# First attention: projections on 512 columns, queries and keys of two heads side by side

## The chip, the cores and the metric

The kernel runs on one core of a Trainium2 chip. The metric is the device time of one execution in microseconds (us). The inputs are in HBM at the start, and the result is in HBM at the end.

## What is computed

Two transformer blocks on 512 tokens of width 1024 in float32. The first block has a differential attention, a SwiGLU, a gated convolution and a second SwiGLU; the second block has windowed attention, an mLSTM and a mixture of experts. The change touches only the first block's attention:

```python
def diff_attention(x, w_qkv, w_o, ...):              # 512 x 1024, H = 8 heads, Dh = 64
    qkv = einsum('bsd,de->bse', x, w_qkv)            # 1024 x 3072: q, k, v
    q, k = partial_rotary(q) * Dh ** -0.5, partial_rotary(k)
    for each block of 128 queries:
        s = einsum('bqhcd,bkhcd->bhcqk', q, k)       # two score maps per head (c = 0, 1)
        p = softmax(where(mask, s, -1e30))           # causal by chunks of 64 keys
        o = einsum('bhqk,bkhe->bqhe', p[c=0] - lam * p[c=1], v)
    o = rms_norm(o, g_sub) * (1 - lam_init)
    return einsum('bse,ed->bsd', o, w_o)
```

## The kernel before

Tokens lie in NT = 4 tiles of P = 128, the width in KD = 8 tiles of 128 (k-tiles). A float32 product is made of three matmuls on rounded parts: `mm3` (lines 129 to 131) multiplies low by high, high by low and high by high. `split` (lines 64 and 65) makes the parts: ScalarE (ACT) writes the high part, VectorE (DVE) the low part.

Weights come through the class `Weights`. A plan lists pieces of 1 MB (a few are smaller) in the order of their use. `load` issues the DMA of a piece on SyncE's queue (SP; line 86), the first piece in two halves of four k-tiles; `prepare` splits it in two halves; `get` hands out a piece and starts what comes next: the following piece is loaded and split, the one after that loaded. Each of `raw`, `whi` and `wlo` has two buffers.

In the projections the tokens are the stationary operand of the matmul and the weights the moving one. `proj_tm` takes a piece of eight k-tiles and 256 columns, and for each token tile runs 8 x 3 matmuls of 256 columns into one PSUM tile `pq`, which ACT then copies out. One token tile of one piece is a *part*, one yield of the generator. `proj_v(c)` projects the values of heads 2c and 2c + 1 (line 383 copies them out), `proj_qk(pair)` first the queries and then the keys of two heads (line 390), each followed by `rotary` on DVE (lines 378 to 380). The tile of the queries has two buffers, that of the keys one.

The attention is a generator, `attend`. A unit is one head and one token tile of queries; there are 32. `head_start(h)` transposes the keys and queries of a head on TensorE (PE; line 397, `ptk` and `ptq`) and splits them; `head_scores` makes both score maps (line 426), their maxima and exponents; `head_turn` transposes the weights (line 449); `head_values` multiplies by the values (line 457); `head_norm` and `head_out` finish a head. Each yield is a *step*; there are 97. After the first two units there are three steps to a unit: the scores of unit i, the values of unit i - 2, the turn of unit i - 1. Counted from unit 0, unit i is thus scored in step 3i - 2 (i of 2 or more), and the scores of a head's third unit also start the next head. Heads 2 and 4 begin with steps 22 and 46 (units 8 and 16), and step 64 is the third unit of head 5 (unit 22). A head has four units, with 128, 256, 384 and 512 keys.

`weave` mixes two generators in given shares. `ATT_WEAVE` has pairs (parts, steps): so many parts of the chain `fill` (the remaining projections, then the first half of the output projection `wo`) are spread among so many steps of `attend`. The framework's scheduler keeps this order as a priority: an instruction that it holds to be ready goes ahead of an earlier one that is not. Inside `manual_schedule` PE keeps the program's order. PSUM has eight banks: four with the tag `g` for projections, four with the tag `m` for the attention. The scratch of `rotary`, the tile `vraw` of `load_vectors` (transposed at line 200 into `vps`) and the tiles of `make_bias` (line 219, `bps`) share the two buffers of the tag `pr1`.

The order before is: v(0), q(0), k(0); the constants (`vps`, `bps`); then attention, woven with q(1), k(1), v(1), q(2), k(2), v(2), q(3), k(3), v(3) and `wo`; then the second half of the output projection and all that follows.

Of the kernel before, what the change touches and what calls it, by code (L numbers as in the profile page):

```python
# [9 lines left out]
F32 = mybir.dt.float32  # L10
# [4 lines left out]
AF = mybir.ActivationFunctionType  # L15
# [6 lines left out]
P = 128  # L22
T = 512
NT = T // P
D = 1024
KD = D // P
# [9 lines left out]
def bcast_rows(ap_1d, n, rows=P):  # L36

    return bass.AP(tensor=ap_1d.tensor, offset=ap_1d.offset, ap=[[0, rows], [1, n]])
# [3 lines left out]
def blocks_kernel(ctx: ExitStack, tc: tile.TileContext, a, out):  # L42
    nc = tc.nc
    dve = nc.vector
    act = nc.scalar
# [12 lines left out]
    def pbank(tag, name="pb"):  # L58
        return psum.tile([P, T], F32, tag=tag, name=name)


    def split(hi, lo, src):

        act.activation(hi, src, AF.Copy)  # L64
        dve.tensor_tensor(out=lo, in0=src, in1=hi.bitcast(F32), op=ALU.subtract)  # L65

    class Weights:
# [9 lines left out]
        def load(self, i):  # L77
            if i < len(self.plan) and i not in self.raw:
                src, kt, cols, gain = self.plan[i]
                raw = ring.tile([P, kt, cols], F32, tag="raw", name="raw")  # L80
                if callable(src):
                    src(raw)
                else:

                    for k0, k1 in ((0, kt // 2), (kt // 2, kt)) if i == 0 else ((0, kt),):
                        nc.sync.dma_start(raw[:, k0:k1], src[k0 * P:k1 * P].rearrange("(k p) c -> p k c", p=P))
                if gain is not None:
                    nc.gpsimd.tensor_tensor(out=raw, in0=raw, in1=gain().unsqueeze(2).to_broadcast([P, kt, cols]),
                                            op=ALU.mult)
                self.raw[i] = raw  # L90
# [21 lines left out]
    W = Weights()  # L112
# [10 lines left out]
    def run(gen):  # L123
        for _ in gen:
            pass

    def mm3(ps, ah, al, bh, bl, start, stop):

        pe.matmul(ps, al, bh, start=start, stop=False)  # L129
        pe.matmul(ps, ah, bl, start=False, stop=False)  # L130
        pe.matmul(ps, ah, bh, start=False, stop=stop)  # L131
# [28 lines left out]
    def load_xt(t):  # L160

        nc.sync.dma_start(X[:, t, :], a["c_xt"][t])
# [4 lines left out]
    def new_xt():  # L167
        return (keep.tile([P, KD, T], F32R, tag="xh", name="xh"),
                keep.tile([P, KD, T], F32R, tag="xl", name="xl"))
# [105 lines left out]
    def plan_out(w, nk, first=None):  # L275
        for half, pp in enumerate(out_parts(nk)):
            for k0, kt in (first if half == 0 and first else pp):
                W.add(w[k0 * P:(k0 + kt) * P, half * 512:(half + 1) * 512], kt, 512)
# [18 lines left out]
    def out_half1(kh, kl, nk, fin, done):  # L297
# [16 lines left out]
        for t in range(NT):  # L314
# [9 lines left out]
            done(t)  # L324
            yield

    def proj_tm(xt, *evacs):

        ws = [W.get() for _ in evacs]
        for t in range(NT):  # L330
            for evac, (wh, wl) in zip(evacs, ws):
                ps = psum.tile([P, 256], F32, tag="g", name="pq")
                for k in range(KD):
                    mm3(ps, xt[0][:, k, t * P:(t + 1) * P], xt[1][:, k, t * P:(t + 1) * P],
                        wh[:, k, :], wl[:, k, :], k == 0, k == KD - 1)
                evac(t, ps)
                yield


    xt = new_xt()  # L340
    wq = a["attn_w_qkv"][0]

    def plan_v(c):
        W.add(wq[:, 2048 + 256 * c:2304 + 256 * c], KD, 256)

    def plan_qk(c):
        W.add(wq[:, 256 * c:256 * c + 256], KD, 256)
        W.add(wq[:, 1024 + 256 * c:1280 + 256 * c], KD, 256)

    ATT_WEAVE = ((12, 21), (12, 24), (10, 21), (2, 9), (4, 9), (4, 12), (7, 2))  # L350
    WO_FIRST = [(0, 4), (4, 2), (6, 1), (7, 1)]
    plan_v(0)
    for c in range(4):
        plan_qk(c)
        if c in (1, 2):
            plan_v(c)
    plan_v(3)
    load_xt(0)
    W.load(0)
    for t in range(1, NT):  # L360
# [2 lines left out]
    with tc.tile_pool(name="att", bufs=2, side="right", reuse_waits="tile") as ap_, \  # L363
            tc.tile_pool(name="att1", bufs=1, side="right", reuse_waits="tile") as a1:
        V = a1.tile([P, NT, D], F32, tag="V", name="V")
        oT = (a1.tile([P, KD, T], F32R, tag="oh", name="oh"), a1.tile([P, KD, T], F32R, tag="ol", name="ol"))
        plan_out(a["attn_w_o"][0], KD, WO_FIRST)

        def rotary(x):

            v = x.rearrange("p t (c e) -> p t c e", e=64)
            x1, x2 = v[:, :, :, 0:8], v[:, :, :, 8:16]
            cc = rope[:, 0].unsqueeze(2).to_broadcast([P, NT, 4, 8])
            ss = rope[:, 1].unsqueeze(2).to_broadcast([P, NT, 4, 8])
            tmp = ap_.tile([P, 4, NT * 4, 8], F32, tag="pr1", name="rt")
            tmp = [tmp[:, i].rearrange("p (t c) e -> p t c e", c=4) for i in range(4)]
            for o, i0, i1 in ((0, x1, cc), (1, x2, ss), (2, x2, cc), (3, x1, ss)):
                dve.tensor_tensor(out=tmp[o], in0=i0, in1=i1, op=ALU.mult)
            dve.tensor_tensor(out=x1, in0=tmp[0], in1=tmp[1], op=ALU.subtract)
            dve.tensor_tensor(out=x2, in0=tmp[2], in1=tmp[3], op=ALU.add)  # L380

        def proj_v(c):
            yield from proj_tm(xt, lambda t, ps: act.activation(V[:, t, 256 * c:256 * c + 256], ps, AF.Copy))

        qk = {}

        def proj_qk(pair):
            for n in "qk":
                x = ap_.tile([P, NT, 256], F32, tag=n, name=n, bufs=2 if n == "q" else 1)
                yield from proj_tm(xt, lambda t, ps: act.activation(x[:, t, :], ps, AF.Copy))  # L390
                rotary(x)
                qk[n, pair] = x

        def head_turned(n, h):
            ps = pbank("m", "pt" + n)
# [118 lines left out]
        lv = ap_.tile([P, 6, 64], F32, tag="pr1", name="lv")  # L514
        for i, n in enumerate(("q1", "k1", "q2", "k2")):
            nc.sync.dma_start(lv[:, i, :], bcast_rows(a["attn_lambda_" + n], 64))
        first_v = proj_v(0)
        for t in range(NT):
            split(xt[0][:, :, t * P:(t + 1) * P], xt[1][:, :, t * P:(t + 1) * P],
                  X[:, t, :].rearrange("p (k e) -> p k e", e=P))  # L520
            load_x(t)
            next(first_v)
        run(first_v)
        act.mul(gsub, gsub, 1.0 - LAM_INIT)
        lp = lv[:, 4:6]
        dve.tensor_tensor(out=lp, in0=lv[:, 0:4:2, :], in1=lv[:, 1:4:2, :], op=ALU.mult)
# [5 lines left out]
        dve.tensor_scalar(out=nlam, in0=nlam, scalar1=LAM_INIT, scalar2=None, op0=ALU.subtract)  # L532

        with tc.manual_schedule(engines={ET.PE}):
            run(proj_qk(0))
            load_vectors(ap_)
            make_bias(ap_)
        wo = out_half0(oT[0], oT[1], KD, norm0.residual, WO_FIRST)
        fill = chain(proj_qk(1), proj_v(1), proj_qk(2), proj_v(2), proj_qk(3), proj_v(3), wo)
        att = attend()  # L540
        for parts, steps in ATT_WEAVE:
            weave((islice(fill, parts), parts), (islice(att, steps), steps))
# [3 lines left out]
        xt = new_xt()  # L546
# [80 lines left out]
    xt = xn  # L627

    with tc.tile_pool(name="cnv", bufs=1, side="right", reuse_waits="tile") as cp, \
# [34 lines left out]
        xt = new_xt()  # L664
# [640 lines left out]
    first = []  # L1305
# [23 lines left out]
    for t in range(NT):  # L1329
        ps = pbank("m", "po")  # L1330
        for i, (wh, wl) in enumerate(wo2):
            for k in range(4):
                kk = 4 * i + k
# [45 lines left out]
    w = r1.tile([P, 2, NT], F32, tag="w", name="w")  # L1379
# [167 lines left out]
    with tc.manual_schedule(engines={ET.PE}):  # L1547
        group_rows(0)
        for e in range(E_ + 1):
            if e > 0:  # L1550
                hT = turned(ss[e - 1])
            g, r = divmod(e, GRP)
# [75 lines left out]
```

## Time and profile before

| | |
|---|---|
| runs (median of 3) | 2211.44 us (2209.98 to 2214.29) |
| profiled execution | 2202.09 us, span 2200.3 us |
| PE, DVE, ACT busy | 94%, 43%, 34% of the span |
| first attention, projections and first half of the output projection | from the start to about 251 us |

The profile is of one execution. A row of the timeline gives start and duration; the ends of matmuls are modelled, so the pace of a stream of matmuls is read from start to start. A row of groups gives total time and mean of one instruction, then the idle time before them and what ended it. A row of stretches gives the length and each engine's busy time in it.

### The profile page before, as it was taken

Reading aid. Unit: us, or ns where it says so; the run is one execution under the profiler, and the core shown is the slowest. Engines: PE = TensorE matmul, PEld = TensorE weight load, DVE = VectorE, ACT = ScalarE, POOL = GpSimd, SP = SyncE. Lnnn points to the kernel's source line nnn. Section 1 sums busy time; section 2 is a strip of 40 time slices with the busy share of each in tenths; the row PEclk is TensorE's granted clock in tenths of the full one; section 3 lists DMA queues with packets and bytes.
Section 4 is the critical chain, followed back from the end, with each engine's and each line's share of the span. In section 5 each row is a group of like instructions: output and inputs, shape, how many; then the busy total and the mean of one; then the engine's idle time right before and its main releaser. Section 6 shows DMA issues by size and latency. Waiting matters only on the chain. (4 is left out here: it accounts for less than half of the span.)

```text
span 2200.3 us, 28119 instructions
## 1 busy us (share of the span) xinstructions
PE 2072.3 (94%) x11131; PEld 1570.6 (71%) x11132; DVE 948.4 (43%) x2042; ACT 749.3 (34%) x1430; POOL 155.8 (7%) x130
## 2 busy tenths in 40 slices
PE   7999999999999999999998899899998998888896
PEld 7998788888888888888887778788884443333332
DVE  3778753332264455333225896577462111111110
ACT  3767532222132223222214355354332221212221
POOL 1000000000000000000002211212100100000101
PEclk9999999999999999999999899999999999999999
DMA  6220233332332223333223211232464999999893
GB/s 217 69 68 20 77 120 102 99 102 87 99 103 96 96 77 118 101 99 103 88 97 104 70 39 39 70 87 91 139 244 180 405 415 412 416 415 415 352 407 108
DMA packets 150166, 354.39 MB, mean 161 GB/s; under 512 B 9892, under 2 KB 103322, under 8 KB 125424
## 3 DMA queue, kind: packets, MB, share of 16 engines
q1 hardware_dynamic: 142864, 334.75, 41.2%
q0 software_dynamic: 7136, 17.39, 3.1%
q8 instruction: 109, 1.79, 0.3%
q14 instruction: 57, 0.47, 0.1%
HBM read 345.77 MB, written 11.30 MB: 162 GB/s over the span
## 5 line engine op out<-in xcount | busy, mean ns | idle before, releaser
L65 DVE TENSOR_TENSOR wlo<-raw,whi 128x1024 fp32r<-128x1024 f32 (+1 forms) x266 | 319.1, 1222 | 445.7 <-ACT whi L64 444.8
L130 PE MATMUL pT<-xl,whi 128*128 128x512 f32 (+1 forms) x1184 | 442.9, 374 | 1.3 <-DVE xl L65 1.3
L131 PE MATMUL pT<-xh,whi 128*128 128x512 f32 (+1 forms) x1184 | 443.1, 374 | 0.0
L129 PE MATMUL pT<-xh,wlo 128*128 128x512 f32 (+1 forms) x1184 | 442.5, 374 | 0.0
L64 ACT ACTIVATE whi<-raw 128x1024 fp32r<-128x1024 f32 (+1 forms) x266 | 258.0, 1004 | 341.1 <-PE po L131 169.0
L1447 PE MATMUL gu<-piece,xg 128*64 128x512 f32 x512 | 236.9, 613 | 18.8 <-DMA piece<-in_w_expert_up 18.7
L130 PEld LDWEIGHTS pT<-xl,whi 128*128 128x128 f32 x1184 | 224.0, 189 | 40.3 <-DVE xl L65 1.7
L129 PEld LDWEIGHTS pT<-xh,wlo 128*128 128x128 f32 x1184 | 223.9, 189 | 38.4
L131 PEld LDWEIGHTS pT<-xh,whi 128*128 128x128 f32 x1184 | 223.8, 189 | 38.3
L1448 PE MATMUL gu<-piece,xg 128*64 128x512 f32 x512 | 237.0, 613 | 0.0
L129 PE MATMUL pq<-whi,xl 128*128 128x256 f32 x608 | 178.5, 294 | 13.7 <-ACT whi L64 11.7
L1447 PEld LDWEIGHTS gu<-piece,xg 128*64 128x64 f32 x512 | 68.4, 140 | 158.0 <-issue 126.6
L130 PE MATMUL pq<-wlo,xh 128*128 128x256 f32 x608 | 175.2, 288 | 2.8 <-DVE wlo L65 2.8
L131 PE MATMUL pq<-whi,xh 128*128 128x256 f32 x608 | 175.4, 289 | 0.0
L1453 DVE SCALAR_TENSOR_TENSOR s<-s,sw,gu 64x512 f32<-64x512 f32 x32 | 35.6, 1114 | 293.1 <-ACT s L1452 293.1
L129 PE MATMUL po<-whi,hl 128*128 128x512 f32 x352 | 139.6, 397 | 0.0
L131 PE MATMUL po<-whi,hh 128*128 128x512 f32 x352 | 139.6, 397 | 0.0
L130 PE MATMUL po<-wlo,hh 128*128 128x512 f32 x352 | 139.6, 397 | 0.0
L1470 PE MATMUL y<-piece,scr 128*64 128x512 f32 x560 | 127.6, 598 | 3.8 <-ACT scr L1461 3.8
L129 PEld LDWEIGHTS pq<-whi,xl 128*128 128x128 f32 x608 | 118.7, 195 | 14.3 <-ACT whi L64 11.3
L130 PEld LDWEIGHTS pq<-wlo,xh 128*128 128x128 f32 x608 | 118.7, 195 | 3.6 <-DVE wlo L65 3.3
L131 PEld LDWEIGHTS pq<-whi,xh 128*128 128x128 f32 x608 | 118.5, 195 | 0.2
(410 smaller groups left out, 2892.7 us busy)
## 6 DMA issues: line engine op xcount, KB each, us to landing
piece<-in_w_expert_gate SPq DMA_DIRECT2D x64, 1024.0 KB, 17.6
piece<-in_w_expert_up SPq DMA_DIRECT2D x64, 1024.0 KB, 19.8
piece<-in_w_expert_down SPq DMA_DIRECT2D x64, 1024.0 KB, 20.2
raw<-in_ffn_w_gate SPq DMA_DIRECT2D x22, 1024.0 KB, 5.3
raw<-in_ffn_w_up SPq DMA_DIRECT2D x22, 1024.0 KB, 5.2
raw<-in_ffn_w_down SPq DMA_DIRECT2D x20, 1024.0 KB, 5.1
raw<-in_w_in SPq DMA_DIRECT2D x19, 1024.0 KB, 5.1
raw<-in_conv_w_in SPq DMA_DIRECT2D x12, 1024.0 KB, 5.1
```

The source lines that it names most:

```text
L64: act.activation(hi, src, AF.Copy)
L65: dve.tensor_tensor(out=lo, in0=src, in1=hi.bitcast(F32), op=ALU.subtract)
L129: pe.matmul(ps, al, bh, start=start, stop=False)
L130: pe.matmul(ps, ah, bl, start=False, stop=False)
L131: pe.matmul(ps, ah, bh, start=False, stop=stop)
L1447: pe.matmul(gu[LOW], xs(k), pc_[2 + k // 4][:, k % 4, :], **st)
L1448: pe.matmul(gu[HIGH], xs(k), pc_[k // 4][:, k % 4, :], **st)
L1453: dve.scalar_tensor_tensor(out=sv, in0=sv, scalar=w, in1=up, op0=ALU.mult, op1=ALU.mult)
L1470: pe.matmul(y[rows], hT[:, f, :], pc_[4 + f // 2][:, f % 2, c * 512:(c + 1) * 512], **st)
```

## The change

A new `proj_wide` replaces `proj_tm` in the first attention. It takes two pieces of four k-tiles and 512 columns, one after the other, and holds four PSUM banks, one for each token tile, through both; a tile is copied out after the second piece. A part is now four k-tiles of one token tile: 4 x 3 matmuls of 512 columns. `proj_v(c)` covers the values of four heads (512 columns); `proj_qk(pair)` has the 256 columns of the queries and the 256 of the keys side by side in a piece, which come by two DMAs; both are copied out in two copies, and both rotaries follow the last token tile. The first projection is that of the queries and keys of heads 0 and 1, and the values of heads 0 to 3 are the first to be woven with the attention. The plan and `ATT_WEAVE` follow. The second block's `proj_tm` is as before.

```diff
@@ -324,6 +324,31 @@
             done(t)
             yield
 
+    def plan_wide(w):
+
+        for k0 in (0, 4):
+            W.add(w[k0 * P:(k0 + 4) * P], 4, 512)
+
+    def proj_wide(xt, evac):
+
+        banks = [None] * NT
+
+        def part(t, j, w):
+            if banks[t] is None:
+                banks[t] = pbank("g", "pq")
+            for k in range(4):
+                kk = 4 * j + k
+                mm3(banks[t], xt[0][:, kk, t * P:(t + 1) * P], xt[1][:, kk, t * P:(t + 1) * P],
+                    w[0][:, k, :], w[1][:, k, :], kk == 0, kk == KD - 1)
+            if j == 1:
+                evac(t, banks[t])
+
+        for j in range(2):
+            w = W.get()
+            for t in range(NT):
+                part(t, j, w)
+                yield
+
     def proj_tm(xt, *evacs):
 
         ws = [W.get() for _ in evacs]
@@ -341,20 +366,26 @@
     wq = a["attn_w_qkv"][0]
 
     def plan_v(c):
-        W.add(wq[:, 2048 + 256 * c:2304 + 256 * c], KD, 256)
+        plan_wide(wq[:, 2048 + 512 * c:2560 + 512 * c])
 
     def plan_qk(c):
-        W.add(wq[:, 256 * c:256 * c + 256], KD, 256)
-        W.add(wq[:, 1024 + 256 * c:1280 + 256 * c], KD, 256)
-
-    ATT_WEAVE = ((12, 21), (12, 24), (10, 21), (2, 9), (4, 9), (4, 12), (7, 2))
+
+        for k0 in (0, 4):
+            def load(raw, k0=k0):
+                for i in range(2):
+                    nc.sync.dma_start(raw[:, :, 256 * i:256 * i + 256],
+                                      wq[k0 * P:(k0 + 4) * P, 1024 * i + 256 * c:1024 * i + 256 * c + 256]
+                                      .rearrange("(k p) c -> p k c", p=P))
+            W.add(load, 4, 512)
+
+    ATT_WEAVE = ((8, 4), (8, 11), (8, 24), (8, 13), (8, 11), (4, 16), (4, 12), (4, 7))
     WO_FIRST = [(0, 4), (4, 2), (6, 1), (7, 1)]
+    plan_qk(0)
     plan_v(0)
-    for c in range(4):
-        plan_qk(c)
-        if c in (1, 2):
-            plan_v(c)
-    plan_v(3)
+    plan_qk(1)
+    plan_qk(2)
+    plan_v(1)
+    plan_qk(3)
     load_xt(0)
     W.load(0)
     for t in range(1, NT):
@@ -380,16 +411,23 @@
             dve.tensor_tensor(out=x2, in0=tmp[2], in1=tmp[3], op=ALU.add)
 
         def proj_v(c):
-            yield from proj_tm(xt, lambda t, ps: act.activation(V[:, t, 256 * c:256 * c + 256], ps, AF.Copy))
+            yield from proj_wide(xt, lambda t, ps: act.activation(V[:, t, 512 * c:512 * c + 512], ps, AF.Copy))
 
         qk = {}
 
         def proj_qk(pair):
-            for n in "qk":
-                x = ap_.tile([P, NT, 256], F32, tag=n, name=n, bufs=2 if n == "q" else 1)
-                yield from proj_tm(xt, lambda t, ps: act.activation(x[:, t, :], ps, AF.Copy))
-                rotary(x)
-                qk[n, pair] = x
+            x = {n: ap_.tile([P, NT, 256], F32, tag=n, name=n, bufs=2 if n == "q" else 1) for n in "qk"}
+
+            def evac(t, ps):
+                for i, n in enumerate("qk"):
+                    act.activation(x[n][:, t, :], ps[:, 256 * i:256 * i + 256], AF.Copy)
+
+                if t == NT - 1:
+                    for n in "qk":
+                        rotary(x[n])
+                        qk[n, pair] = x[n]
+
+            yield from proj_wide(xt, evac)
 
         def head_turned(n, h):
             ps = pbank("m", "pt" + n)
@@ -514,13 +552,12 @@
         lv = ap_.tile([P, 6, 64], F32, tag="pr1", name="lv")
         for i, n in enumerate(("q1", "k1", "q2", "k2")):
             nc.sync.dma_start(lv[:, i, :], bcast_rows(a["attn_lambda_" + n], 64))
-        first_v = proj_v(0)
+        first = proj_qk(0)
         for t in range(NT):
             split(xt[0][:, :, t * P:(t + 1) * P], xt[1][:, :, t * P:(t + 1) * P],
                   X[:, t, :].rearrange("p (k e) -> p k e", e=P))
             load_x(t)
-            next(first_v)
-        run(first_v)
+            next(first)
         act.mul(gsub, gsub, 1.0 - LAM_INIT)
         lp = lv[:, 4:6]
         dve.tensor_tensor(out=lp, in0=lv[:, 0:4:2, :], in1=lv[:, 1:4:2, :], op=ALU.mult)
@@ -532,11 +569,11 @@
         dve.tensor_scalar(out=nlam, in0=nlam, scalar1=LAM_INIT, scalar2=None, op0=ALU.subtract)
 
         with tc.manual_schedule(engines={ET.PE}):
-            run(proj_qk(0))
+            run(first)
             load_vectors(ap_)
             make_bias(ap_)
         wo = out_half0(oT[0], oT[1], KD, norm0.residual, WO_FIRST)
-        fill = chain(proj_qk(1), proj_v(1), proj_qk(2), proj_v(2), proj_qk(3), proj_v(3), wo)
+        fill = chain(proj_v(0), proj_qk(1), proj_qk(2), proj_v(1), proj_qk(3), wo)
         att = attend()
         for parts, steps in ATT_WEAVE:
             weave((islice(fill, parts), parts), (islice(att, steps), steps))
```

## Rows read from the trace of the kernel before

**Rows 1.** The page's first part: engine, busy us (share) and instructions.

```profile
PE 2072.3 (94%) x11131; PEld 1570.6 (71%) x11132; DVE 948.4 (43%) x2042; ACT 749.3 (34%) x1430; POOL 155.8 (7%) x130
```

**Rows 2.** Stretches: us, busy PE, PEld, DVE, ACT, POOL; clock, DMA, GB/s.

```profile
50.16:251.27 201.11, 193.41 (x1426) 177.52 (x1425) 161.14 (x520) 136.13 (x375) 1.03 (x2) 1.00 0.18 59
```

**Rows 3.** Timeline of PE from 24 us: start, duration, line, operation.

```profile
24.04 0.28 PE L129 MATMUL pq<-whi,xl 128*128 128x256 f32 x1
...
30.04 0.28 PE L131 MATMUL pq<-whi,xh 128*128 128x256 f32 x1
```

**Rows 4.** Timeline of PE from 213 us.

```profile
213.68 0.40 PE L130 MATMUL po<-wlo,oh 128*128 128x512 f32 x1
...
216.66 0.40 PE L131 MATMUL po<-whi,oh 128*128 128x512 f32 x1
```

**Rows 5.** Groups by shape, 0 to 420 us: count, busy, mean ns, idle.

```profile
L129 PE MATMUL pq<-whi,xl 128*128 128x256 f32 x384 | 112.0, 292 | 11.7 <-ACT whi L64 11.7
```

**Rows 6.** Groups by shape on DVE and ACT, 58 to 246 us.

```profile
L65 DVE TENSOR_TENSOR wlo<-raw,whi 128x1024 fp32r<-128x1024 f32 x18 | 21.9, 1221 | 2.3 <-ACT whi L64 2.1
L378 DVE TENSOR_TENSOR rt<-q,rope 128x128 f32<-128x128 f32 x12 | 2.8, 284 | 0.1
...
L451 ACT ACTIVATE aT<-pta 128x512 f32<-128x512 f32 x8 | 4.8, 600 | 0.3 <-PE pta L449 0.2
L383 ACT ACTIVATE V<-pq 128x256 f32<-128x256 f32 x12 | 4.6, 385 | 5.4 <-PE pq L131 5.4
```

**Rows 7.** Waits of SyncE queue, 50 to 200 us: total, times, longest.

```profile
SPq L86 <- DVE wlo L65: 62.3, 4, 18.6
```

**Rows 8.** Timeline of all engines from 10 us.

```profile
10.55 2.00 ACT L64 ACTIVATE whi<-raw 128x1024 fp32r<-128x1024 f32 x2 [3.74 <-DMA raw<-in_attn_w_qkv]
...
11.65 0.58 PE L129 MATMUL pq<-whi,xl 128*128 128x256 f32 x1 [11.65 <-ACT whi L64]
```

**Rows 9.** DMA issues to 2.0 and 2.5 us: KB, median landing.

```profile
raw<-in_attn_w_qkv SPq DMA_DIRECT2D x1, 512.0 KB, 8.8
...
raw<-in_attn_w_qkv SPq DMA_DIRECT2D x2, 512.0 KB, 9.0
```

**Rows 10.** Timelines of DVE, POOL, ACT, PE, 39 to 58 us.

```profile
39.06 0.90 DVE L378 TENSOR_TENSOR rt<-q,rope 128x128 f32<-128x128 f32 x4 [6.14 <-ACT q L390]
...
40.55 0.21 POOL L189 MEMSET vraw<- 128x128 f32 x1 [20.53 <-DVE q L380]
...
50.16 0.38 ACT L390 ACTIVATE k<-pq 128x256 f32<-128x256 f32 x1 [2.50 <-PE pq L131]
...
56.08 0.27 PE L200 MATMUL vps<-ident,vraw 128*128 128x128 f32 x1
...
57.95 0.66 PE L397 MATMUL ptk<-ident,k 128*128 128x128 f32 x4
```

**Rows 11.** Timeline of PE: steps 22, 46 and 64.

```profile
104.79 0.56 PE L426 MATMUL sc<-kT,qT 128*128 128x128 f32 x4
...
156.76 0.56 PE L426 MATMUL sc<-kT,qT 128*128 128x128 f32 x4
...
191.74 0.94 PE L426 MATMUL sc<-kT,qT 128*128 128x384 f32 x4
```

**Rows 12.** Stretches: steps 22-45, 64-96 and the last twelve.

```profile
104.79:156.76 51.97, 50.54 (x407) 48.72 (x405) 41.72 (x128) 34.77 (x97) 0.00 (x0) 1.00 0.19 62
...
191.70:246.60 54.90, 51.69 (x318) 42.98 (x317) 46.57 (x172) 38.02 (x110) 0.00 (x0) 1.00 0.15 49
...
229.15:246.60 17.45, 15.10 (x87) 11.89 (x86) 14.13 (x59) 11.30 (x32) 0.00 (x0) 1.00 0.37 122
```

**Rows 13.** Groups by shape on PE, 191.7 to 246.6 us.

```profile
L131 PE MATMUL pq<-whi,xh 128*128 128x256 f32 x25 | 7.3, 292 | 0.0
L130 PE MATMUL pq<-wlo,xh 128*128 128x256 f32 x25 | 7.2, 287 | 0.0
L129 PE MATMUL pq<-whi,xl 128*128 128x256 f32 x24 | 6.9, 289 | 0.0
```

## The prediction, made before the change was run

> **What bounds the kernel now.** I read the page first: TensorE (PE) is busy for 94% of the span and VectorE (DVE) for 43% [rows 1]. The change touches only the first attention, so the next view is the table by stretch: between the end of the first key projection (50.16 us) and the start of the second half of the output projection (251.27 us) PE is busy for 193.4 of 201.1 us and DVE for 161.1 [rows 2]. PE sets the time there, and at most 7.7 us of it can be won by closing holes, but DVE at 80% stands close behind. "Busy" hides how closely the matmuls follow each other, so the third view is the timeline, read from start to start. With 256 columns, 50 intervals from 24.04 to 30.04 us give 0.120 us for one matmul [rows 3]. With 512 columns and the same roles (tokens stationary, weights moving), 13 intervals of the output projection from 213.68 to 216.66 us give 0.229 us, and these lie between attention work, as the changed ones will [rows 4].
>
> **The wider matmuls.** The projections of q, k and v have 3 x 384 = 1152 matmuls of 256 columns (one of three like groups stands in [rows 5]): 1152 x 0.120 = 138.2 us. The change makes them 576 of 512 columns: 576 x 0.229 = 131.9 us. Saved: 6.3 us of PE time, all of it on the path if PE stays the bound. A part of eight k-tiles on one token tile was 24 x 0.120 = 2.88 us; the new part of four k-tiles is 12 x 0.229 = 2.75 us.
> On this point a page speaks against the change: the Trainium skill (TensorE: Matmul & The Clock Gate, Back-to-back issue gap) lists 262 cycles for 256 columns and 518 for 512 at full clock, so two narrow ones cost only 6 cycles more than a wide one; by that the saving would be an estimated 576 x 2.5 ns = 1.4 us. The measured starts differ from both entries, and they decide.
>
> **Copies out of PSUM and loads.** V goes out in 8 copies of 512 columns in place of 16 of 256: 16 x 0.385 = 6.2 us of ScalarE (ACT) becomes about 8 x 0.60 = 4.8 us, by the nearest copy of that width, 0.600 [rows 6]; q and k keep 32 copies of 256. ACT has more room than DVE throughout, so nothing is counted (0 to -1.4 us if it did bind). Weights are 12 MB in 12 pieces as before. Eight of those pieces come by two DMAs instead of one; SyncE's queue waits for a free buffer anyway, up to 18.6 us a time [rows 7], and a piece is needed every 11 us (4 x 2.75), as before every 11.5. Counted 0; without that cover it would be one issue, some 0.4 us, a piece.
>
> **The start.** The first matmul waits for the first weight split, which starts at 10.55 us when the first 512 KB has landed [rows 8]. These 512 KB held k-tiles 0 to 3; now the first split needs the q half and the k half, both 512 KB. The first landed 8.8 us after an issue at 1.70; the two together have 9.0 in the middle, so the second took about 9.2 from an issue near 2.2 and landed at 11.4 [rows 9]. Cost +0.9 us, between 0 and +1. Token tiles and second weight piece are needed at the same pace as before, so nothing else is late.
>
> **The order at the start.** v(0), 96 narrow matmuls, leaves the time before 50.16 us: q and k of heads 0 and 1 end near 50.16 - 11.5 - 1.0 + 0.9 = 38.6 us. PE loses nothing, since v(0) follows as filler (8 x 2.75 = 22 us). Both rotaries now come after the last part, one behind the other: 6 x 0.284 = 1.7 us each on DVE [rows 6]. The tile `vraw` reuses the q rotary's scratch and is cleared at 40.55 us now; then come POOL's loads, the transpose of `vps` at 56.08 and the keys' first transpose at 57.95 [rows 10]. Queued behind them on PE is the whole attention. With the q rotary ending near 41, `vps` and attention stay at about 56 to 58, with v(0) under them where the queries and keys of heads 2 and 3 are now. Counted 0; if the filler ran out it would be the 1.7 us of the second rotary for each of three later pairs, 5 us, since a pair's keys are now asked for one step after its last part.
>
> **The dense stretch.** I count the attention by its steps (97; unit i from the third on is scored in step 3i - 2). Steps 22 to 45 ran from 104.79 to 156.76 us [rows 11], with 12 projection parts: 51.97 - 12 x 2.88 = 17.4 us of PE for 24 steps and two head starts. DVE was busy 41.7 us in it, 80% [rows 12]. After the change steps 16 to 39, also 24 steps with two head starts, share PE with 8 parts only: 17.4 + 22.0 = 39.4 us. DVE has one weight split less, 2 x 1.22 us [rows 6]: 41.7 - 2.4 = 39.3 us. DVE would have to be busy 100%. At the 90% which I take as its practical limit (an estimate of mine, between the 85% reached under a well filled PE in [rows 12], its row of steps 64 to 96, and 100%) the stretch takes 43.6 us: +4.2 us. But steps 40 to 63 have 16 parts: PE 61.4 us, DVE about 44. PE can run those parts early, as now it runs some 7 us of the next pair between 50.16 and 57.95 us, before attention starts [rows 10]. So 0 to +4.2; I take +1.5, nearer to full cover.
>
> **The end.** This is the largest term. Steps 64 to 96 run from 191.74 to 246.60 us [rows 11, 12]: 54.9 us, PE busy 51.7, DVE 46.6 (85%). In it lie 74 matmuls of the last queries, keys and values (25, 25 and 24 of the three products) [rows 13], 74 x 0.120 = 8.9 us. After the change all of these are done before step 64, and only the output projection is left as filler, which can't start before its heads are finished. PE alone would need 54.9 - 8.9 = 46.0 us. DVE's work stays 46.6 us: it would have to be above 100% busy. At 90% the stretch takes 51.8 us, 5.8 over PE's; at 97%, 48.0, +2.0; and where PE already had room, in the last 17.45 us, DVE reached only 14.1, 81%, because each unit is a chain of scores, maximum, exponent, sum and turn [rows 12]. At that share nothing would be won in this stretch: 54.9 us, +8.9. So +2.0 to +8.9; I take +4.5 (50.5 us, DVE 92%), nearer to the low end since the longest chains stand only in its last third, which is not thinned out.
>
> **Sum.** -6.3 + 0.9 + 1.5 + 4.5 = +0.6 us. The profiled execution took 2202.09 us, 9.4 us under the median of the runs, 2211.44; I carry the difference over unchanged: 2202.7 by the profiled execution, 2212.0 by the runs. About 0.2%, 4.4 us, is what a measurement of this kernel tells from no change.
>
> **Rivals.**
> *PE stays the bound everywhere.* For it: PE is the busier engine in each of [rows 12], and its holes are few. Then only the start takes something from the saving: -6.3 + 0.9 = -5.4, 2206.0 us.
> *The attention's chain becomes the bound in the thinned-out end.* The place is steps 64 to 96, the price the whole 8.9 us of lost filler, and it decides if DVE can't get past 85% of that stretch; the same limit would show in steps 16 to 39 with the 4.2. For it: the 81% of the last stretch. Against: there the tail of the last head is mixed in. -6.3 + 0.9 + 4.2 + 8.9 = +7.7, 2219.1 us.
> *The wide matmul is not cheaper.* If 512 columns next to attention cost 0.240, twice the narrow one, the first term is gone: +6.9, 2218.3 us. Against it stand the 13 intervals, which were measured in such a place; the tile that is written and the operands have the same shapes.
>
> **How the numbers follow.** The forecast has 0.45, PE everywhere 0.27, the chain at the end 0.23, no cheaper matmul 0.05. The first holds from about -4 to +4; the second is all of faster, the last two all of slower: faster 0.27, same 0.45, slower 0.28. The forecast's own range is 2208 to 2216. For 8 in 10 the range must take in most of the second and third case: down to -7.7, which is the saving of the matmuls and of the copies with no loss at all, and up to the chain's +7.7 and a little of the rotaries' 5. The range is 2204 to 2220 us.
>
> **What would show it.** Right: starts of the wide projection matmuls 0.229 us apart; the first matmul near 12.5 us; step 64 (the scores of head 5's third unit, with the start of head 6 behind them) near 193 to 200 us and from there to the end of step 96 about 50 us with DVE above 90% and PE below 90%. The second half of the output projection then starts near 252 us, as now at 251.27. If it starts near 246, PE was the bound; near 259, the chain. After it nothing should move: the rest has the same instructions. The prediction is wrong if PE waits long for the rotaries or for `vps`, if the order on PE puts attention behind filler where DVE has room, or if the rest of the kernel moves by more than 2 us.

## The result and the profile after

| | before | after |
|---|---|---|
| runs, interleaved (medians of 15) | 2205.97 us | 2219.69 us |
| profiled execution, span | 2202.09, 2200.3 us | 2222.33, 2220.5 us |
| ratio after / before | | 1.0054 (1.0039 to 1.0069) |

The kernel became 0.54% slower, about 12 us; the forecast was no change, +0.6 us. The page's first part shows PE busy 9 us longer, although it has 576 matmuls less (10555 in place of 11131, [rows 1]): busy time grows when the clock falls (a 128x512 matmul is listed with 0.63 us at 53 to 56 us, where the clock is low, and with 0.39 at 45.04), and 98 us of this span were granted at the lower clock, 57 of the span before.

```profile
PE 2081.2 (94%) x10555; PEld 1546.7 (70%) x10556; DVE 950.8 (43%) x2042; ACT 747.3 (34%) x1422; POOL 157.1 (7%) x130
...
PEclk9999899999999999999999899999998999999999
```

The fifth slice of the PEclk line (222 to 278 us) is an 8, where the kernel before had a 9. The end of the first attention lies there. The stretches say what happened (columns: us; busy PE, PEld, DVE, ACT, POOL with counts; clock; DMA share; GB/s). First after:

```profile
38.60:57.21 18.61, 16.12 (x59) 11.65 (x58) 7.11 (x17) 5.38 (x9) 4.82 (x10) 0.82 0.21 64
...
100.82:200.79 99.97, 98.45 (x522) 79.96 (x521) 80.85 (x258) 67.88 (x189) 0.00 (x0) 1.00 0.16 51
200.79:254.60 53.81, 44.97 (x230) 33.72 (x228) 43.70 (x146) 35.24 (x103) 0.00 (x0) 0.93 0.12 45
254.60:259.47 4.87, 1.99 (x6) 1.34 (x7) 3.34 (x19) 1.30 (x4) 0.00 (x0) 0.50 0.69 215
259.47:288.20 28.73, 28.72 (x125) 23.12 (x123) 20.48 (x52) 11.11 (x21) 0.00 (x0) 0.92 0.12 37
```

and of before, from step 64 to the first matmul behind the last turn (`pto`) of head 7, and as much behind it:

```profile
191.74:251.27 59.53, 54.72 (x331) 45.11 (x330) 50.56 (x188) 39.20 (x114) 0.00 (x0) 1.00 0.19 61
...
251.27:280.00 28.73, 28.59 (x146) 23.28 (x146) 22.93 (x60) 14.69 (x26) 0.00 (x0) 1.00 0.15 43
```

Two places lose. Between 38.60 and 57.21 us, where PE had been full, it idles 2.5 us and the mean clock is 0.82. From step 64 (200.79 us; 191.74 in [rows 11]) to the first matmul behind the last `pto` (259.47; 251.27 before), PE idles 53.81 + 4.87 - 44.97 - 1.99 = 11.7 us against 59.53 - 54.72 = 4.8 before, and the clock falls there too. The steps between (16 to 63, 100.82 to 200.79 us) are full, at full clock. In the first 300 us the granted clock of after is at its lower level (1.2 GHz) four times, from 49.2 (6.8 us), 226.7 (3.4), 243.7 (3.4) and 254.0 us (10.2); in that profile of before it is at full speed (2.4 GHz) throughout.

**The first place**, on PE's timeline of after (start, duration, operation; in brackets the idle time and what ended it):

```profile
45.04 0.39 PE L129 MATMUL pq<-whi,xl 128*128 128x512 f32 x1
47.53 0.30 PE L200 MATMUL vps<-ident,vraw 128*128 128x128 f32 x1 [2.11 <-issue]
...
48.91 1.66 PE L219 MATMUL bps<-oh,tab 33*8 33x512 f32 x2 [0.38 <-DMA oh<-in_c_t]
50.50 1.12 PE L435 MATMUL ptk<-ident,k 128*128 128x128 f32 x4
...
53.12 0.63 PE L129 MATMUL pq<-whi,xl 128*128 128x512 f32 x1
53.55 0.63 PE L130 MATMUL pq<-wlo,xh 128*128 128x512 f32 x1
...
56.29 0.39 PE L131 MATMUL pq<-whi,xh 128*128 128x512 f32 x1
56.52 0.39 PE L129 MATMUL pq<-whi,xl 128*128 128x512 f32 x1
```

and on DVE and POOL ahead of it:

```profile
38.17 0.90 DVE L409 TENSOR_TENSOR rt<-q,rope 128x128 f32<-128x128 f32 x4 [6.57 <-ACT q L423]
...
39.39 0.28 DVE L411 TENSOR_TENSOR q<-rt 128x128 f32<-128x128 f32 x1
...
39.74 0.21 POOL L189 MEMSET vraw<- 128x128 f32 x1 [19.97 <-DVE q L411]
...
42.84 1.00 POOL L195 DMA_DIRECT2D vraw<-in_norm_g  x2
```

The wide part holds queries and keys to its end, so the rotary of the queries, whose scratch `vraw` reuses, is done at 39.67 us. Then POOL clears `vraw` and issues its loads; the last two go out at 42.84 and 43.34 us and took 2.9 and 4.0 us to land, so the later is there at 47.3, 0.2 us before `vps` starts. PE's order has `vps` 34 wide matmuls (7.8 us) behind the first projection; the clearing comes 5.7 us ahead of that place, and before it was 15.5 us [rows 10]. So PE stands for 2.11 and 0.38 us. Behind that come 6.8 us at the lower clock, where the starts are 0.43 us apart, not 0.23.

**The second place** is the end; the waits of PE from 12 to 300 us (us in all, times, longest), leaving out the start:

```profile
PE vps L200 <- issue: 2.1, 1, 2.1
PE pov L495 <- ACT pr L471: 1.9, 2, 1.6
PE pov L495 <- ACT aT L489: 1.8, 2, 1.6
PE pto L512 <- DVE o L505: 1.6, 1, 1.6
PE po L129 <- DVE ol L514: 1.3, 1, 1.3
PE pta L487 <- DVE pr L478: 1.1, 1, 1.1
PE pto L512 <- ACT pr L471: 1.0, 1, 1.0
```

The values `pov` wait for the exponent `pr` and the copied turn `aT`, the turn `pta` for DVE's `pr`, `pto` for the normed `o`: links of the chain of one unit, one after the other, with no filler left. DVE is busy 43.70 of 53.81 us, 81%. And the low clock reaches into work that PE has in plenty, the output projection behind the last `pto`:

```profile
259.40 0.41 PE L512 MATMUL pto<-ident,o 128*128 128x128 f32 x1
259.47 0.78 PE L131 MATMUL po<-whi,oh 128*128 128x512 f32 x1
260.05 0.63 PE L129 MATMUL po<-whi,ol 128*128 128x512 f32 x1
260.47 0.63 PE L130 MATMUL po<-wlo,oh 128*128 128x512 f32 x1
...
263.46 0.63 PE L131 MATMUL po<-whi,oh 128*128 128x512 f32 x1
263.89 0.54 PE L129 MATMUL po<-whi,ol 128*128 128x512 f32 x1
```

The second half of the output projection starts only with the last of these rows: the twelve matmuls from 258.38 to 263.46 us are the last k-tile of the first half, three for each token tile. In the kernel before it starts at 250.72 us, ahead of the last `pto`, so that its matmuls fill a part of that wait:

```profile
250.72 0.39 PE L129 MATMUL po<-whi,ol 128*128 128x512 f32 x1
...
251.18 0.33 PE L474 MATMUL pto<-ident,o 128*128 128x128 f32 x1
```

**The account.** Counting DVE's instructions from the end, the same one stands 12.1 us later in after than in before from 290 to some 1180 us. Worked out: -6.3 (matmuls), +0.8 (first matmul at 12.44 in place of 11.65), +2.5 and half of 6.8 at `vps` (+5.9), +6.9 of idle time in the end; that is +7.3, or +6.0 with the 1.3 us that PE idles less in the other stretches. The 6.1 us left are near what 17.0 us at half clock in the end can cost: at most 7.0, half of the 14.0 us of them in which PE was busy. Behind 1180 us this pair of profiles parts by another 8 us, with the same instructions. The clock has a part in that (behind 320 us, 74 us at the lower level against 57), but it isn't shown to be all: the next execution of before also has 74 us there and parts by only 2.7 (last experiments).

### The profile page after: what moved, and what is told of

It reads as the page before. It is cut to its first block, busy times and chain, and to the rows that moved or that the text cites. A ratio compares the mean times of both kernels' runs of the same rounds, so it can differ in the third digit from the quotient of the medians.

```text
span 2220.5 us, 26988 instructions
## 1 busy us (share of the span) xinstructions
PE 2081.2 (94%) x10555; PEld 1546.7 (70%) x10556; DVE 950.8 (43%) x2042; ACT 747.3 (34%) x1422; POOL 157.1 (7%) x130
## 5 line engine op out<-in xcount | busy, mean ns | idle before, releaser
L1484 PE MATMUL gu<-piece,xg 128*64 128x512 f32 x512 | 240.2, 621 | 17.0 <-DMA piece<-in_w_expert_up 16.8
L1485 PE MATMUL gu<-piece,xg 128*64 128x512 f32 x512 | 240.2, 621 | 0.0
L129 PE MATMUL pq<-whi,xl 128*128 128x256 f32 (+1 forms) x416 | 146.3, 352 | 14.4 <-ACT whi L64 12.4
L130 PE MATMUL pq<-wlo,xh 128*128 128x256 f32 (+1 forms) x416 | 143.7, 346 | 7.0 <-DVE wlo L65 7.0
L131 PE MATMUL pq<-whi,xh 128*128 128x256 f32 (+1 forms) x416 | 143.0, 344 | 0.0
L1489 ACT ACTIVATE s<-gu 64x512 f32<-64x512 f32 x32 | 34.3, 1070 | 237.9 <-PE gu L1485 237.9
L88 POOL TENSOR_TENSOR raw<-raw,vecs 128x2048 f32<-128x2048 f32 (+1 forms) x20 | 72.8, 3643 | 556.9 <-DMA raw<-in_w_in 472.9
L1507 PEld LDWEIGHTS y<-piece,scr 128*64 128x64 f32 x560 | 39.9, 137 | 82.5 <-issue 75.5
```

The costliest lines, as they stand in the source:

```text
L1484: pe.matmul(gu[LOW], xs(k), pc_[2 + k // 4][:, k % 4, :], **st)
L1485: pe.matmul(gu[HIGH], xs(k), pc_[k // 4][:, k % 4, :], **st)
L1489: act.activation(sv, gate, AF.Silu)
L1507: pe.matmul(y[rows], hT[:, f, :], pc_[4 + f // 2][:, f % 2, c * 512:(c + 1) * 512], **st)
```

## The experiments

The theory A: two causes, each about half: (1) `vps` made late by the shared scratch, with the clock behind it; (2) the thinned-out end. Below, "the stage" is the place of that DVE instruction at some 700 us against the first profile of before: after has +12.1. It is read from one execution each.

**1. The constants in tiles of their own.** After, with `vraw` and `oh` in another buffer than the rotary's scratch.

```diff
-        vraw = pool.tile([P, P], F32, tag="pr1", name="vraw")
+        vraw = pool.tile([P, P], F32, tag="pr0", name="vraw")
...
-        oh = pool.tile([33, T], F32, tag="pr1", name="oh")
+        oh = pool.tile([33, T], F32, tag="pr0", name="oh")
```

> The changed kernel, with the tiles vraw and oh in the buffers of the tag pr0, which are free at the start, so that their loads no longer wait for the rotaries. Theory A (three terms: wide matmuls -6.3 us, a stall of PE before vps with half a clock behind it +5.9 us, a thinned-out end with idle PE and half a clock +12 us): the first attention ends some 6 us earlier than in the changed kernel, the kernel is about 6 us slower than before instead of 12, PE has no wait at vps, and the clock stays at 1.00 from 45 to 60 us. Rival B (the attention's own chain sets the end, whatever happens at the start): PE's wait at vps goes, but idle time at the end grows by as much; 10 to 12 us slower than before.

Measured: 1.0029 (1.0016 to 1.0041), 2214.73 against 2209.23 us; the stage +6.4. The timeline of PE in it:

```profile
38.13 0.39 PE L131 MATMUL pq<-whi,xh 128*128 128x512 f32 x1
38.36 0.27 PE L200 MATMUL vps<-ident,vraw 128*128 128x128 f32 x1
38.56 1.02 PE L219 MATMUL bps<-oh,tab 33*8 33x512 f32 x2
```

No wait, and PE is full at full clock from 38 to 58 us. Against after that is 0.25% or 5.5 us of the times, with an uncertainty of some 4, and 5.7 of the stage, near the 5.9 of the account. The profile shows cause (1) taken away; whether the times show it too is asked again with experiment 7. The other half remains, and so do the waits of the end.

**2. Values of heads 4 to 7 late again.** After, but these values in two narrow projections, those of heads 6 and 7 behind the last queries and keys, as before.

```diff
...
-    ATT_WEAVE = ((8, 4), (8, 11), (8, 24), (8, 13), (8, 11), (4, 16), (4, 12), (4, 7))
+    ATT_WEAVE = ((8, 4), (8, 11), (8, 24), (4, 13), (8, 11), (4, 12), (4, 9), (4, 12), (7, 2))
...
-    plan_v(1)
+    plan_vn(2)
     plan_qk(3)
+    plan_vn(3)
...
```

> The changed kernel, but the values of heads 4 to 7 are projected as before the change, on 256 columns for two heads at a time, and those of heads 6 and 7 after the last queries and keys, beside steps 64 to 75. Theory A: the end has its filler again, so idle time and half clock after step 64 mostly go (-10 to -12 us), 96 pairs of narrow matmuls cost 96 x 0.011 = +1.1 us, the stall at vps stays: about 2 us slower than before. Rival C (the loss lies in the dense steps 16 to 39, or in the order of the whole attention): the end changes little, 8 to 12 us slower than before.

Measured: 0.9993 (0.9976 to 1.0011), 2207.04 us; the stage +2.7. The stretches with filler in the end again:

```profile
200.00:230.00 30.00, 28.67 (x172) 23.46 (x171) 25.13 (x80) 23.10 (x68) 0.00 (x0) 1.00 0.03 10
230.00:252.00 22.00, 18.05 (x95) 14.13 (x94) 16.85 (x69) 12.54 (x37) 0.00 (x0) 0.95 0.41 132
```

The wait at `vps` is still there (1.8 us). So giving the end its filler back gains 9.4 us of the stage, and of the times 0.61%, some 13 us with an uncertainty of 5. Cause (2) is the larger one. (This execution also waited 2.0 us for the second weight piece, at 27.71 and 28.97 us, which that of after did not.) It takes the width of these values with it: what is shown is the place and the width together, but 192 narrow matmuls for 96 wide cost PE 1.0 us, not gain it.

**3. Wide queries and keys alone.** Before, its order, only the queries and keys with 512 columns.

```diff
...
-        W.add(wq[:, 256 * c:256 * c + 256], KD, 256)
-        W.add(wq[:, 1024 + 256 * c:1280 + 256 * c], KD, 256)
...
+            W.add(load, 4, 512)
...
     plan_v(0)
     for c in range(4):
         plan_qk(c)
         if c in (1, 2):
             plan_v(c)
     plan_v(3)
...
-                yield from proj_tm(xt, lambda t, ps: act.activation(x[:, t, :], ps, AF.Copy))
...
+            yield from proj_wide(xt, evac)
...
```

> The kernel before, with queries and keys alone on 512 columns; values on 256, the order of the projections and the weave as before. Theory A: 384 pairs x 0.011 = -4.2 us; the end keeps its filler; but both rotaries of heads 0 and 1 now come late, vraw waits for them, and PE stalls at vps as in the changed kernel (2 to 6 us with the clock behind it): between 2 us faster and 2 us slower than before. Rival D (the stall comes from the new order, queries and keys ahead of the values): no stall, 4 us faster than before. Rival E (wide matmuls save nothing beside attention): 0 to 6 us slower.

Measured: 1.0010 (0.9996 to 1.0024), 2212.17 us; the stage +2.3. The wait comes with the wide queries and keys, whatever goes first:

```profile
57.79 0.39 PE L129 MATMUL pq<-whi,xl 128*128 128x512 f32 x1
60.16 0.30 PE L200 MATMUL vps<-ident,vraw 128*128 128x128 f32 x1 [1.98 <-issue]
```

With it, and 3.4 us at the lower clock behind it, the wide queries and keys alone bring nothing that can be measured.

**4. The order alone.** Before with 256 columns, queries and keys of heads 0 and 1 first and v(0) as filler.

```diff
...
-    ATT_WEAVE = ((12, 21), (12, 24), (10, 21), (2, 9), (4, 9), (4, 12), (7, 2))
+    ATT_WEAVE = ((4, 4), (9, 11), (3, 6), (12, 24), (10, 21), (2, 9), (4, 9), (4, 12), (7, 2))
...
+    plan_qk(0)
     plan_v(0)
-    for c in range(4):
+    for c in range(1, 4):
         plan_qk(c)
-        if c in (1, 2):
-            plan_v(c)
-    plan_v(3)
+        plan_v(c)
...
-        first_v = proj_v(0)
+        first = proj_qk(0)
...
-        fill = chain(proj_qk(1), proj_v(1), proj_qk(2), proj_v(2), proj_qk(3), proj_v(3), wo)
+        fill = chain(proj_v(0), proj_qk(1), proj_v(1), proj_qk(2), proj_v(2), proj_qk(3), proj_v(3), wo)
...
```

> The kernel before with the new order alone: q and k of heads 0 and 1 first, v(0) as the first filler of the attention; all matmuls on 256 columns, q and k one after the other, v(3) late as before. Theory A: the query rotary runs during the key projection, so vraw is loaded in time and PE does not stall at vps; the end keeps its filler; TensorE is as busy as before: within 2 us of before. Rival D (the order itself costs, by the early attention or by the constants behind the first projection): 5 us slower or more.

Measured: 0.9999 (0.9983 to 1.0015), 2206.8 against 2209.72 us; the stage -1.4, with no wait at `vps`. Here the rotary of the queries runs while the keys are projected. So the order costs nothing that can be measured; the late rotary does.

**5 and 6. Wide queries and keys, or the second experiment's order, with own buffers.** Experiments 3 and 2 with the two lines of experiment 1.

> The same as e3_wide_qk_alone, with vraw and oh in the free buffers of pr0. Theory A: no stall at vps, the end as before: 384 x 0.011 = 4.2 us faster than before. Rival E (wide matmuls save nothing beside attention): within 1 us of before.

Measured (from 3): 0.9977 (0.9963 to 0.9991), 2204.47 us; the stage +0.7.

> e4_late_narrow_values with vraw and oh in the free buffers of pr0: both causes of theory A taken away. Theory A: 6.3 - 1.1 us of matmuls saved, neither stall nor thin end: about 5 us faster than before, up to 7. Rival B (the attention's chain gives the time back at the end): as e4_late_narrow_values, 1 to 2 us faster than before.

Measured (from 2): 0.9981 (0.9963 to 1.0000), 2205.03 us; the stage -2.5. Against experiment 1, which has the same buffers, the second of them repeats cause (2): 0.48%, 10.6 us of the times, 8.9 of the stage. Both are faster than before, near what was expected, and both seemed to show the saving of the wide matmuls, until the next one.

**7. Before, with own buffers.** Only the two lines of experiment 1, in the kernel before.

> The kernel before, with vraw and oh in the free buffers of pr0 and nothing else. Theory A: PE does not wait at vps in the kernel before, so there is nothing to win: within 1 us of before, and the gain of e6_wide_qk_own_buffers is that of the wide matmuls. Rival: the earlier start of the attention alone is worth 3 to 5 us.

Measured: 0.9971 (0.9958 to 0.9983), 2203.62 us; the stage 0.0. Theory A did not expect that: `vps` does not wait in the profile of before, and yet the kernel gains 6.4 us. The rival on record, that the earlier start of the attention is worth 3 to 5 us, fits the time but not the profile: `vps` starts at 50.47 us in place of 56.08, and the stage, from one execution, shows nothing of it. It takes away the reading of 5 and 6: their gain over before is no larger than that of the buffers alone, so that the wide matmuls are worth anything in the total is not shown (the three agree within 0.1%, and a few us either way stay open). It weakens experiment 1 as well: in the times, the same two lines gain 5.5 us where `vps` waits and 6.4 where it doesn't, so what the wait costs is read from profiles alone, 2.5 us of idle time and the lower clock behind it where that comes.

**8. More filler in the end.** Experiment 1, with the first 48 matmuls of the output projection done twice, 11.0 us more for PE.

```diff
...
-                for k in range(kt):
+                for i, k in enumerate(list(range(kt)) * (twice if seen == 0 else 1)):
...
-        wo = out_half0(oT[0], oT[1], KD, norm0.residual, WO_FIRST)
+        wo = out_half0(oT[0], oT[1], KD, norm0.residual, WO_FIRST, twice=2)
...
```

> e1_own_buffers with useless work at its thin end: the first 48 matmuls of the output projection (k-tiles 0 to 3, steps 64 to 79) are run twice, the second time over the first, so the result is the same. That is 48 x 0.229 = 11.0 us more of TensorE's work. Theory A (TensorE idles there, and falls to half clock after it): the added work costs less than half, 0 to 5 us over e1_own_buffers, and the half clock near 221 us is gone. Rival (TensorE is still the bound there): 9 to 11 us over e1_own_buffers, 15 to 17 over before.

Measured: 1.0037 (1.0021 to 1.0054), 2216.7 us: 0.08%, 1.8 us, above experiment 1, with an uncertainty of some 4.5. By the times most of 11 us of added PE work was free, as it must be if the chain sets the end. The one profile does not bear that out so well: its stage is at +14.3, 7.9 behind experiment 1. From 200 to 225 us in experiment 1, then here:

```profile
200.00:225.00 25.00, 22.57 (x116) 16.76 (x114) 21.15 (x68) 17.93 (x52) 0.00 (x0) 0.93 0.13 43
```

```profile
200.00:225.00 25.00, 24.88 (x130) 20.13 (x129) 15.98 (x54) 12.88 (x41) 0.00 (x0) 1.00 0.00 1
```

PE is full and at full clock, but DVE gets 16.0 us of work done in place of 21.2: put where it was, the added work also held up the attention. How much was hidden is open between the two readings.

**9 to 12. Before, experiment 7 and after once more**, one execution each, to see why experiment 7 gained.

> The kernel before once more, to see the trace of a second execution: the profile of before is faster than nearly all its timed runs, and e8_before_own_buffers, whose attention ends at the same time in that profile, was 0.29% faster in the timed runs. Theory F (the constants' loads are not always in time: PE does stall at vps or bps in most executions of before): a wait of 1 to 4 us of PE at vps or bps, near 56 us, with half a clock behind it, and the attention ends 2 to 6 us later than in the first profile. Theory G (the end of the attention falls to half clock in most executions): no wait there, a half clock between 240 and 260 us. If neither shows, the 0.29% stays open.

> The kernel before a third time. As b1_before_again: theory F a wait at vps or bps near 56 us, theory G a half clock between 240 and 260 us.

> e8_before_own_buffers a second time. Theory F: no wait at vps or bps, and the attention ends where it did in its first profile, within 1 us. Theory G: the half clock near 245 us comes and goes here as in before.

> The changed kernel a second time. Theory A: the wait at vps (about 2 us) and the half clock behind it come again, so do PE's idle times and half clock at the end; the attention ends 9 to 13 us later than in the first profile of before. If the waits are an accident of one execution, they are not there.

Measured: before 2210.09 and 2212.05 us, experiment 7 2202.25, after 2213.33. Theory F does not hold: `vps` doesn't wait. Theory G's low clock in the end comes in one of the two executions of before (3.4 us from 252.2 us in the first) and in this one of experiment 7 (6.8 us from 244.8, its stage +1.3). But in both executions of before PE also waits near 28 us, which no theory had; in the first of the two:

```profile
28.33 0.39 PE L129 MATMUL pq<-whi,xl 128*128 128x256 f32 x1 [2.52 <-ACT whi L64]
29.59 0.39 PE L130 MATMUL pq<-wlo,xh 128*128 128x256 f32 x1 [0.87 <-DVE wlo L65]
...
30.17 0.28 PE L131 MATMUL pq<-whi,xh 128*128 128x256 f32 x1
30.29 0.38 PE L129 MATMUL pq<-whi,xl 128*128 128x256 f32 x1
30.46 0.42 PE L130 MATMUL pq<-wlo,xh 128*128 128x256 f32 x1
30.68 0.41 PE L131 MATMUL pq<-whi,xh 128*128 128x256 f32 x1
```

The split of the second weight piece waits for its DMA: here the split starts at 27.22 us, in the profile on which the prediction rests at 22.59. PE stands for 2.5 us, then runs 3.4 us at the lower clock (starts 0.21 apart, not 0.12). The other execution has 2.2 us and again 3.4; the stage is +5.3 and +3.0. So the profile of before that was read for the prediction was a lucky one. In experiment 7 the same place is

```profile
26.57 0.28 PE L129 MATMUL pq<-whi,xl 128*128 128x256 f32 x1
27.45 0.39 PE L130 MATMUL pq<-wlo,xh 128*128 128x256 f32 x1 [0.60 <-DVE wlo L65]
27.67 0.28 PE L131 MATMUL pq<-whi,xh 128*128 128x256 f32 x1
```

and no low clock follows, in neither of its two executions. What differs there is POOL's queue: with free buffers the loads of `vraw` and `oh` go out from 2.80 us, and the first reload of `X` at 10.89 in place of 8.36. That a later reload lets the weights land in time fits, but was not tried by itself, and experiment 5, which has that queue order too, did wait there once (2.02 us at 28.01, with 3.4 us of low clock behind it). So the gain of experiment 7 is measured, its cause only argued; of its 6.4 us the stages show 2.1 (mean 0.7 in its two executions, 2.8 in the three of before).

After, in its second execution, waits 2.0 us at `vps` as in the first, and in the end at the same places:

```profile
PE po L129 <- DVE ol L514: 2.3, 2, 1.3
PE vps L200 <- issue: 2.0, 1, 2.0
PE pov L495 <- ACT pr L471: 1.9, 2, 1.6
PE pov L495 <- ACT aT L489: 1.8, 2, 1.6
```

This time the clock does not fall behind `vps`, only twice in the end (from 238.1 and 251.8 us, 6.8 each), and the stage is at +8.0, below the 9 expected as its least. So the waits repeat, the clock does not. With these executions the account reads: the stage of after +12.1 and +8.0, mean 10.0; of before 0, +5.3 and +3.0, mean 2.8; difference 7.3. Behind the stage after lost another 8.2 and 3.3 us, before 0, 2.7 and 7.0: 5.7 against 3.2, +2.5. Together 9.8, inside the 8.6 to 15.2 us of the timed ratio; how much lies behind the stage can't be settled from so few executions.

## Why the prediction was right in its range and wrong in its steps

The 2219.7 us lie in the stated range, 2204 to 2220 us, but that is luck: the range was built on 2211.44 us for the kernel before, which took 2205.97 in the runs beside the changed one. The change itself, about 12 us, is beyond what the range leaves above that base, 8.6 us, and far from the sum's +0.6. Two steps failed, the order at the start and the end.

**"The wider matmuls", -6.3: right in the rows.** The starts are 0.23 us apart where the clock is full (56.29 and 56.52 above). The Trainium skill's 262 and 518 cycles (TensorE: Matmul & The Clock Gate, Back-to-back issue gap), given there for a single matmul in isolation, 0.109 and 0.216 us at 2.4 GHz, both lie below the rows (0.120 in [rows 3], and 0.229), the narrow one as far as the wide one; that difference for each matmul, halved in number, is what the estimate of 1.4 us from that page lacks. In the total the saving was never isolated (experiment 7).

**"The start", +0.9: right for the profile it was read from.** The first matmul began 0.8 us later (12.44 in both executions of after; in the other two of before it began at 10.92 and 10.80 us, so that +1.6 was possible), and the new order alone cost nothing (experiment 4).

**"The order at the start", counted 0: this step failed, +5.9 in the profile.** Of that 2.5 us are idle time, which the second execution of after repeats (2.4), and 3.4 the low clock, which it doesn't. It saw that the rotary comes late, that `vraw` shares its scratch and what is queued behind. But it held `vps` at 56 to 58 us, where [rows 10] has it, as if that time came from the data. It came from the order on PE. With the wide filler in front that order put `vps` 34 matmuls behind the projection, at 45.4 us, and the last load of `vraw` landed only just ahead of 47.53. The step asked how late the data would be and not how early PE would be made to ask for them. Its price for the failure ("5 us" if filler ran out) was near, by another mechanism.

**"The dense stretch", +1.5: too high by that much.** Steps 16 to 63 took 99.97 us, PE alone was worked out at 39.4 + 61.4 = 100.8. The parts of steps 40 to 63 were pulled forward, the full cover that was given as the lower bound.

**"The end", +4.5: mis-sized.** The stretch of step 64 to 96 was to take 50.5 us with DVE at 92%; it took 53.8, with DVE at 81%: +7.8 over PE's 46.0 in place of +4.5, and the low clock into the projection behind it came on top. That is the rival in which the attention's chain becomes the bound, near its +8.9 (giving the filler back gained 9.4 us of the stage in experiment 2), and its row, the 81% of the last 17.45 us [rows 12], came back for the whole stretch. The prediction put it aside because the tail of the last head was mixed in. That the share agrees so closely is in part luck: the step kept DVE's work at 46.6 us, but only 43.7 fell into the stretch (8 instructions that norm an `o`, 15 before); 46.6 in 53.8 us would be 87%. The sign for the end can't be read as it was meant: 251.27 us is the first matmul behind the last `pto`, and the second half had begun at 250.72. After has it at 263.89 us, later than any case had it, with the time lost at `vps` in it; in experiment 1, without that, it is 258.29, near the 259 of the chain. The rival's total, 2219.1, was also the nearest of the four; but its +7.7 looks nearer than it is by the lower time of before, it had 4.2 us from the dense stretch, which did not come, and nothing from `vps`, which did.

**What no step had: the clock.** Thinned-out stretches were priced as idle time alone. The end held 17.0 us at 1.2 GHz, in part where PE had full work, and 6.8 more stood behind `vps`: up to 10.4 us (half of the 20.8 in which PE was busy at that level), beside 9.4 us of added idle time in the two places.

**"After it nothing should move":** single profiles part by 2.7 to 8 us behind the stage, those of before too; the step's bound of 2 us was narrower than one execution can tell.

**Versions below both in time:** before with the constants in their own buffers (0.9971), and experiments 5 and 6 (0.9977, 0.9981; the interval of the last reaches 1.0000). Their intervals overlap; which is best is not settled.

## What to carry to other kernels

Work that is taken out of a dense engine may be the filler that keeps a chain of dependent steps covered: before moving it forward, take the busy share that the chain reaches where it already runs bare, price the whole thinned stretch at that share too, with the work that will really fall into it, and then the clock behind the holes. A moved step moves the instructions queued around it too: ask for every tile that shares a buffer with it both when its data come and where the consumer now stands in its engine's order. And read the kernel before in more than one execution: a single profile can be the lucky one.

## What the runs showed of the hardware

The clock fell to 1.2 GHz behind waits of 1.8 to 2.5 us in an otherwise full PE (behind `vps`, 6.8 us at that level in after and 3.4 in experiments 2 and 3; behind the late weight piece, 3.4), so that such a wait cost up to an estimated 5.9 us in all (2.5 idle and half of 6.8). It is not fixed: the same 2.0 us at `vps` had no low clock behind it in after's second execution. Behind the bare end (PE busy 2.0 of 4.9 us) it stayed low for 4.7 us after full work had begun again. And the landing of one 1 MB weight piece at the start, with the DMA engines full (their busy share is 1.0 from 22 to 28 us), moved its split from 22.6 to 27.2 us between executions of one and the same kernel.
